# First products into the second SwiGLU in float32 from unsplit operand and weights

## The chip, the cores and the metric

The kernel runs on one core of one Trainium2 chip. The metric is the device time of one execution in microseconds, from its start to the end of the last instruction. Several runs of one kernel are given by their median. The profile is of one execution and its times count from the start of its span.

## The reference

Two layers (DEPTH = 2) work on x with 256 positions and 1024 channels. Each layer has three sublayers: a SwiGLU, three token mixers in parallel (RWKV-7, Hyena, SSD) that are merged by gates and one output projection, and a second SwiGLU. Around each stands a modulated input and a LayerNorm of the scaled residual:

```
h = x * (1 + scale) + shift            # scale, shift, gate from c, by linear layers (adaLN)
y = sublayer(h)
x = LayerNorm(ALPHA * x + gate * y)

def swiglu(h, wi, wo):                 # wi 1024 x 5632, wo 2816 x 1024
    gu = h @ wi
    return (jax.nn.silu(gu[..., :D_FF]) * gu[..., D_FF:]) @ wo
```

Everything is float32 in and out.

## The kernel before, in words

**Tiles.** Activations lie transposed: channels on the 128 partitions, positions along the row, so x is eight tiles of 128 x 256 (index m as an output, k as an input). Weights come from memory in units of [128 x 1024] float32, 512 KB: eight 128 x 128 blocks, one for each k, and a unit gives one output tile. wi's units are called here 0, 1, 2, ... in the order in which they are used: (j, q) with j the column block and q = 0 for the silu half, 1 for the other. They are issued on SyncE's queue (SP) into a ring of four raw buffers.

**Two ways of multiplying float32.** `unit` (L321) splits what has been loaded: ScalarE (ACT) writes the rounded high part (whi), VectorE (DVE) the rest (wlo), both as float32r in rings of five halves of 512 columns; the activation is split the same way (hhi, hlo). `mm3` (L341) then makes a product of three matmuls, high by high, high by low, low by high. `plain` (L311) only loads the unit, and `product` hands the float32 tiles to one matmul, which the trace shows as two records. The first `ahead` units have their own tiles in either case: wq (plain), or wqh and wql (split); the others go through the raw ring. A split unit frees its raw buffer as soon as both halves are split; a plain unit keeps it until its last product.

**The transition between two sublayers** is what the change touches. `ln_begin` (L477) starts a LayerNorm. `ln_put` (L536) is called for each of the eight output tiles of the sublayer: r = gate * psum + xa on DVE, its square on ACT, running sums racc and lsa on DVE, and at the end four matmuls of ones that add racc, lsa and the last tile and its square over the channels (tile pss). `u_put` (L500) scales r by the next sublayer's factor. `early` (L510) multiplies that not yet normalised operand with the first four units (NE = 4) of the next sublayer's first weight, in 258 columns: 256 positions and two columns that give what the mean and the shift contribute. `ln_end` (L570) takes the statistics: mean and variance (lmu, lv), the logarithm and exponential for the reciprocal root (two ACT functions with a table load between them), then for each tile r * lv, the modulated hf, and its split hhi, hlo; the units from 4 on use these. `early_end` (L525) corrects the four early results with mean and reciprocal root on DVE, and from them come the first silu (sg) and the first free psd bank.

**Which way at which transition.** From a SwiGLU into the mixers the early products are plain float32 (operand `um`). Into the second SwiGLU of a layer (from the mixers) and into the next layer's first SwiGLU they are split (operands `uh`, `ul`).

**The end of the mixers** (`mixers`, L1371): the first two branches' outputs are merged under weights pab and gates gi, in the midst of which `ln_begin` is called and the first wout unit loaded (L1428 to L1430); then a loop over eight wout units with `dense` and `ln_put` (L1435 to L1439), then `early` with the first wi units (L1440), then `ln_end` (L1442). NPRE = 1, so only unit 0 has a tile of its own. Units 4 and 5 go into psm banks, units 6 and 7 need the psd banks that early results hold until sg has read them.

**Order.** The order of the instructions on each engine, SP's queue among them, is set by a scheduler that simulates the program with its own costs; the program gives only dependences and priorities, so a change in one function moves instructions elsewhere.

Of the kernel before, what the change touches and what calls it, by code (L numbers as in the profile page):

```python
# [211 lines left out]
class Builder:  # L212
# [264 lines left out]
    def ln_begin(self, l, sub):  # L477
        self.lsub = (l, sub)
        self.nxt = (l, sub + 1) if sub < 2 else (l + 1, 0)
        self.r = self.lt("r", (8, 256))  # L480
        if (l, sub) == (0, 0):
            self.xa = self.x0
        else:
            xa = self.xa = self.lt("xa", (8, 256))
            for m in range(0, 8, 4):
                self.dma(xa[:, m:m + 4, :], self.xd[:, m:m + 4, :])
        if self.nxt in self.mods:
            mod = self.mods[self.nxt]
            if self.nxt[1] == 1:
                self.uh = self.lt("um", (8, 258))  # L490
                self.ts(self.uh[:, :, 256], mod[:, 24:32], -1.0, MUL)
                self.ts(self.uh[:, :, 257], mod[:, 32:40], 1.0, MUL)
                return
            self.uh, self.ul = (self.lt(n, (8, 258), dt=F32R) for n in ("uh", "ul"))
            ab = self.lt("uab", (8, 2))
            self.ts(ab[:, :, 0], mod[:, 24:32], -1.0, MUL)
            self.ts(ab[:, :, 1], mod[:, 32:40], 1.0, MUL)
            self.split(self.uh[:, :, 256:258], self.ul[:, :, 256:258], ab[:])

    def u_put(self, m):  # L500

        if self.nxt in self.mods:
            assert (*self.nxt, 0) in self.done and (*self.nxt, 1) in self.done
            a, hi = self.mods[self.nxt][:, 24 + m:25 + m], self.uh[:, m, 0:256]
            self.act(hi, self.r[:, m, :], AF.Identity, scale=a)
            if self.nxt[1] == 1:
                return
            self.stt(self.ul[:, m, 0:256], self.r[:, m, :], a, hi.bitcast(F32), MUL, SUB)

    def early(self, units, ahead):  # L510


        banks = [self.bank("d", 4)[:, 0:258] for _ in units]
        plain = self.nxt[1] == 1
        load = self.plain if plain else self.unit
        ws = [load(u, ahead=ahead if i < ahead else None) for i, (_, u) in enumerate(units)]
        xs = [self.uh[:, k, :] if plain else (self.uh[:, k, :], self.ul[:, k, :]) for k in range(NT)]
        for ks in (range(7), (7,)):
            for i in range(0, len(units), 2):
                for k in ks:  # L520
                    for p, w in zip(banks[i:i + 2], ws[i:i + 2]):
                        self.product(p, w, k * 128, xs[k], k == 0, k == 7)
        self.adv = [(key, p) for (key, _), p in zip(units, banks)]
# [972 lines left out]
```

## Time and profile before

| | |
|---|---|
| median of 3 runs | 1669.35 us (1665.41 to 1672.22) |
| the profiled execution | 1675.59 us |
| its span | 1673.7 us |
| mean granted clock of TensorE | 0.975 |
| busy: PE, DVE, ACT, POOL | 94%, 69%, 48%, 16% |
| from the mixers into the second SwiGLU, layer 0 | about 636 to 690 us of the span |
| the same, layer 1 | about 1445 to 1491 us |

PE is the engine of the matmuls. Its records end later than the next begins, so the distance of two starts, and not the duration shown, is what a matmul costs in a row of them. A number in square brackets behind a row of the timeline is the idle time of its engine just before it, with what ended it. PEclk is the granted clock as a share of 2.4 GHz.

### The profile page before, as it was taken

To read this page: it belongs to the slowest core of one execution; us is meant where nothing else is said; L and a number is where in the kernel's file an instruction comes from. 1 tells how busy PE (TensorE), PEld (TensorE's weight loads), DVE (VectorE), ACT (ScalarE), POOL (GpSimd) and SP (SyncE) were. 2 spreads that over 40 slices of the span, in tenths; PEclk is the share of its full clock that TensorE was granted. 3 is DMA by queue.
4 is the path that set the end of the run, shared out by engine and by line. 5 is a ranking of instruction groups with operands and counts; after the bars stand their busy time and mean duration, and the time that the engine had idled before them with its cause. 6 is when DMAs were issued, how large, how long until landed. Compare 5 with 4: busy or idle time off the path is not lost.

```text
span 1673.7 us, 31929 instructions
## 1 busy us (share of the span) xinstructions
PE 1569.5 (94%) x12118; PEld 1424.0 (85%) x12118; DVE 1150.0 (69%) x2326; ACT 801.3 (48%) x1566; POOL 267.4 (16%) x376
## 2 busy tenths in 40 slices
PE   5999999879998988899999999998999998989996
PEld 2999998768877878899999999877787787989996
DVE  6788856636446677888888887467454557876665
ACT  2655545423243535655575555452424342665554
POOL 0000013567001001100030000348620100030001
PEclk9999999989999999899999999998999999989998
DMA  9898834554548754788869986345555655666663
GB/s 376 305 324 280 282 123 155 129 127 144 169 150 288 242 170 151 282 304 295 266 220 366 315 307 199 120 106 138 156 151 158 223 188 194 189 198 221 222 177 93
DMA packets 157879, 355.74 MB, mean 213 GB/s; under 512 B 55900, under 2 KB 75805, under 8 KB 157470
## 3 DMA queue, kind: packets, MB, share of 16 engines
q1 hardware_dynamic: 157726, 353.71, 64.3%
q8 instruction: 95, 1.56, 0.4%
q14 instruction: 58, 0.48, 0.1%
HBM read 332.11 MB, written 18.91 MB: 210 GB/s over the span
## 4 chain that ended last, share of the span: by engine, by line
PE 66%; DVE 10%; POOL 9%; DMA 7%; ACT 4%; issue 3%; SPq 1%; DVEq 0%; ACTq 0%; POOLq 0%
PE psd L293 57%; PE psm L293 5%; PE pss L293 4%; POOL arena L921 3%; POOL arena L919 3%; DVE arena L282 3%; DVE arena L290 2%; DVE wlo L309 1%; SPq L296 1%; DMA arena<-in_ada 1%; ACT L279 1%; DMA gi<-gate 1%; DMA ada_raw<-in_ada 1%; ACT arena L279 1%; DMA raw<-in_pab 1%
## 5 line engine op out<-in xcount | busy, mean ns | idle before, releaser
L279 ACT ACTIVATE whi<-raw 128x512 fp32r<-128x512 f32 x608 | 370.6, 618 | 328.8 <-PE psd L293 268.2
L309 DVE TENSOR_TENSOR wlo<-raw,whi 128x512 fp32r<-128x512 f32 x608 | 405.1, 676 | 135.1 <-ACT whi L279 120.2
L293 PE MATMUL psd<-hhi,raw 128*128 128x256 f32 x1856 | 435.8, 389 | 0.7 <-DVE arena L290 0.7
L293 PEld LDWEIGHTS psd<-hhi,raw 128*128 128x128 f32 x1856 | 348.9, 192 | 63.3 <-issue 11.6
L293 PE MATMUL psd<-hhi,whi 128*128 128x256 f32 x1360 | 385.4, 285 | 9.9 <-DVE r L290 4.9
L293 PE MATMUL psd<-hhi,wlo 128*128 128x256 f32 x1360 | 384.6, 284 | 1.3 <-DVE wlo L309 1.3
L293 PE MATMUL psd<-hlo,whi 128*128 128x256 f32 x1360 | 385.5, 284 | 0.0
L293 PEld LDWEIGHTS psd<-hhi,whi 128*128 128x128 f32 x1360 | 262.0, 193 | 11.8 <-ACT sg L279 4.6
L293 PEld LDWEIGHTS psd<-hhi,wlo 128*128 128x128 f32 x1360 | 261.9, 193 | 1.6 <-DVE wlo L309 1.5
L293 PEld LDWEIGHTS psd<-hlo,whi 128*128 128x128 f32 x1360 | 262.5, 193 | 0.1
L293 PE MATMUL psd<-alo,whi 128*128 128x256 f32 x704 | 198.7, 282 | 0.0
L293 PE MATMUL psd<-ahi,wlo 128*128 128x256 f32 x704 | 197.8, 281 | 0.0
L293 PE MATMUL psd<-ahi,whi 128*128 128x256 f32 x704 | 197.4, 280 | 0.0
L581 POOL TENSOR_TENSOR r<-r,lmu 128x256 f32<-128x256 f32 x36 | 31.2, 899 | 1020.7 <-ACT lmu L279 841.3
L290 DVE SCALAR_TENSOR_TENSOR ada_raw<-ada_raw,cond 128x1024 f32<-128x1024 f32 x104 | 127.1, 1222 | 20.3 <-DMA ada_raw<-in_ada 20.1
L293 PEld LDWEIGHTS psd<-ahi,wlo 128*128 128x128 f32 x704 | 134.0, 190 | 0.3
L293 PEld LDWEIGHTS psd<-alo,whi 128*128 128x128 f32 x704 | 132.8, 189 | 0.2
L293 PEld LDWEIGHTS psd<-ahi,whi 128*128 128x128 f32 x704 | 132.2, 188 | 0.1
L293 PE MATMUL pss<-arena 128*64 128x128 f32 (+5 forms) x486 | 101.7, 385 | 26.9 <-ACT arena L279 8.6
L279 ACT ACTIVATE arena<-arena 128x512 f32<-128x512 f32 (+4 forms) x108 | 65.8, 619 | 102.5 <-DVE arena L290 35.6
L293 PEld LDWEIGHTS pss<-arena 128*64 128x64 f32 (+3 forms) x486 | 65.4, 195 | 52.1 <-issue 21.0
L293 PE MATMUL psm<-arena 32*32 32x32 f32 (+6 forms) x664 | 64.5, 263 | 28.1 <-DVE arena L290 12.6
(228 smaller groups left out, 2169.9 us busy)
## 6 DMA issues: line engine op xcount, KB each, us to landing
raw<-in_wi SPq DMA_DIRECT2D x176, 512.0 KB, 4.6
raw<-in_win SPq DMA_DIRECT2D x118, 512.0 KB, 3.8
ada_raw<-in_ada SPq DMA_DIRECT2D x104, 512.0 KB, 5.5
raw<-in_wo SPq DMA_DIRECT2D x64, 512.0 KB, 3.8
arena<-in_ada SPq DMA_DIRECT2D x32, 512.0 KB, 5.9
raw<-in_wo SPq DMA_DIRECT2D x32, 384.0 KB, 3.7
raw<-in_pab SPq DMA_DIRECT2D x24, 512.0 KB, 4.3
raw<-in_wout SPq DMA_DIRECT2D x16, 512.0 KB, 4.2
```

The lines of the kernel that those rows point to most:

```text
L279: return self.nc.scalar.activation(out=out, in_=in_, func=func, **k)
L282: return self.nc.vector.tensor_tensor(out=out, in0=a, in1=b, op=op)
L290: return self.nc.vector.scalar_tensor_tensor(out=out, in0=a, scalar=s, in1=b, op0=op0, op1=op1, **k)
L293: return self.nc.tensor.matmul(out, lhsT, rhs, start=start, stop=stop, **k)
L296: self.nc.sync.dma_start(out, in_)
L309: return self.act(hi, src, AF.Copy), (eng or self.nc.vector).tensor_tensor(out=lo, in0=src, in1=hi.bitcast(F32), op=SUB)
L581: x = sub_(out=r[:, m, :], in0=r[:, m, :], in1=mu[:], op=SUB)
L919: g.tensor_tensor(out=tv, in0=zw[:, j + 1:32, j:j + 1].to_broadcast([64, n, j]), in1=zw[:, j:j + 1, 0:j].to_broadcast([64, n, j]), op=MUL)
L921: g.tensor_tensor(out=zw[:, j + 1:32, 0:j], in0=zw[:, j + 1:32, 0:j], in1=tv, op=ADD)
```

## The change

At three places `nxt[1] == 1` (the next sublayer is the mixers) becomes true also for `nxt[1] == 2` (the next is the second SwiGLU). The transition into the next layer's first SwiGLU stays split.

```diff
@@ ln_begin
             mod = self.mods[self.nxt]
-            if self.nxt[1] == 1:
+            if self.nxt[1]:
                 self.uh = self.lt("um", (8, 258))
@@ u_put
             self.act(hi, self.r[:, m, :], AF.Identity, scale=a)
-            if self.nxt[1] == 1:
+            if self.nxt[1]:
                 return
             self.stt(self.ul[:, m, 0:256], self.r[:, m, :], a, hi.bitcast(F32), MUL, SUB)
@@ early
-        plain = self.nxt[1] == 1
+        plain = self.nxt[1] > 0
         load = self.plain if plain else self.unit
```

So in each layer the 32 early products (four units by eight k) become one float32 matmul each in the place of three float32r, ACT's eight and DVE's eight splits of half a unit and DVE's eight `ul` are gone, unit 0 is loaded into a wq tile, and units 1 to 3 stay in raw buffers until their last early product. `ln_end` splits h for the second SwiGLU as before.

**PE, layer 0, where the statistics stand among the early products.** psd 6440 to 6443 (before) and 6428 to 6431 (after) are the four early results, pss the statistics. Before, with 53 rows of early matmuls ahead of these, each a third of a product:

```order
L293 MATMUL pss_6394<-racc_6130,onesd 128x256
L293 MATMUL psd_6442<-uh_5685,wlo_6471 128x258
L293 MATMUL psd_6440<-uh_5685,wqh_6450 128x258
L293 MATMUL psd_6441<-uh_5685,whi_6460 128x258
L293 MATMUL psd_6442<-uh_5685,whi_6470 128x258
L293 MATMUL pss_6395<-lsa_6131,onesd 128x256
L293 MATMUL pss_6394<-r_5681,onesd 128x256
L293 MATMUL psd_6443<-uh_5685,whi_6476 128x258
L293 MATMUL psd_6443<-ul_5686,whi_6476 128x258
```

The statistic of lsq follows eight rows further on, and more early products after it. After, from the last wout product on:

```order
L293 MATMUL psd_6428<-um_5685,wq_6432 128x258 x5
L293 MATMUL psd_6429<-um_5685,raw_6434 128x258 x5
L293 MATMUL psd_6428<-um_5685,wq_6432 128x258
L293 MATMUL psd_6429<-um_5685,raw_6434 128x258
L293 MATMUL psd_6430<-um_5685,raw_6436 128x258 x3
L293 MATMUL pss_6383<-racc_6126,onesd 128x256
L293 MATMUL psd_6428<-um_5685,wq_6432 128x258
L293 MATMUL pss_6384<-lsa_6127,onesd 128x256
L293 MATMUL pss_6383<-r_5681,onesd 128x256
L293 MATMUL pss_6384<-lsq_6423,onesd 128x256
L293 MATMUL psd_6429<-um_5685,raw_6434 128x258
L293 MATMUL psd_6431<-um_5685,raw_6438 128x258 x3
```

All four statistics now stand behind 16 of the 32 products; the other 16 follow them, and then the products of unit 4 and 5.

**DVE, layer 0, from the last r to the first hlo.** wlo are splits of weights, lv the variance, r<-r,lv the normalised tile, hf and hlo the modulated input and its low part. Before:

```order
L309 TENSOR_TENSOR wlo_6731<-raw_6728,whi_6730 128x512
L290 SCALAR_TENSOR_TENSOR ul_5686<-r_5681,mod_5065,uh_5685 128x256
L290 SCALAR_TENSOR_TENSOR lv_6582<-pss_6395,lmu_1110_6580 128x256
L581 TENSOR_TENSOR r_5681<-r_5681,lmu_6581 128x256 x2
L309 TENSOR_TENSOR wlo_6735<-raw_6728,whi_6734 128x512
L282 TENSOR_TENSOR r_5681<-r_5681,lv_6582 128x256 x2
L287 TENSOR_SCALAR hf_6602<-r_5681,mod_5065 128x256
L282 TENSOR_TENSOR r_5681<-r_5681,lv_6582 128x256
L309 TENSOR_TENSOR wlo_6745<-raw_6742,whi_6744 128x512
L309 TENSOR_TENSOR wlo_6749<-raw_6742,whi_6748 128x512
L309 TENSOR_TENSOR wlo_6812<-raw_6809,whi_6811 128x512
L309 TENSOR_TENSOR hlo_6605<-hf_6602,hhi_6604 128x256
```

After:

```order
L290 SCALAR_TENSOR_TENSOR r_5681<-psd_6397,mod_938,xa_5682 128x256
L309 TENSOR_TENSOR wlo_6637<-raw_6634,whi_6636 128x512
L309 TENSOR_TENSOR wlo_6641<-raw_6634,whi_6640 128x512
L290 SCALAR_TENSOR_TENSOR lv_6474<-pss_6384,lmu_1094_6472 128x256
L581 TENSOR_TENSOR r_5681<-r_5681,lmu_6473 128x256 x2
L309 TENSOR_TENSOR wlo_6704<-raw_6701,whi_6703 128x512
L282 TENSOR_TENSOR r_5681<-r_5681,lv_6474 128x256 x2
L287 TENSOR_SCALAR hf_6494<-r_5681,mod_5065 128x256
L282 TENSOR_TENSOR r_5681<-r_5681,lv_6474 128x256
L309 TENSOR_TENSOR hlo_6497<-hf_6494,hhi_6496 128x256
```

The last ul and the splits of unit 4 have gone from here, those of unit 5 stand ahead of lv and the first of unit 6 behind the mean's subtraction, and no split of weights stands between r<-r,lv and the first hlo any more; unit 4 is split two r earlier.

**SP, layer 1, in the merge of the branches.** pab are the merge's weights, gi its gates, xa the residual. Before:

```order
L296 DMA xa_14744<-xd_12109 128x1024
L296 DMA gi_14621<-gate_13556 128x256
L296 DMA xa_14744<-xd_12109 128x1024
L296 DMA raw_14860<-in_pab 128x1024
L296 DMA gi_14637<-gate_13556 128x256
L296 DMA raw_14904<-in_pab 128x1024
L296 DMA gi_14663<-gate_13556 128x256
```

After:

```order
L296 DMA xa_14636<-xd_12001 128x1024
L296 DMA gi_14513<-gate_13448 128x256
L296 DMA xa_14636<-xd_12001 128x1024
L296 DMA wq_15386<-in_wi 128x1024
L296 DMA raw_14748<-in_pab 128x1024
L296 DMA gi_14529<-gate_13448 128x256
L296 DMA raw_14792<-in_pab 128x1024
L296 DMA gi_14555<-gate_13448 128x256
```

Unit 0's load stands ahead of a pab; before it stood behind the last wout load, just ahead of units 1 to 3. In layer 0 it has moved to the same region, behind the pab that stands after xa and ahead of a gi. Further on the raw ring is used in another way: units 4, 5 and 6 go one after the other through the one raw buffer that units 1 to 3 leave, and units 7 and 8 are loaded into theirs after the last early products, on SP behind three and six of the eight stores xd<-r.

## Rows read from the trace of the kernel before

**Rows 1.** The page: busy time, and the chain that ended last, by line.

```profile
PE 1569.5 (94%) x12118; PEld 1424.0 (85%) x12118; DVE 1150.0 (69%) x2326; ACT 801.3 (48%) x1566; POOL 267.4 (16%) x376
...
PE psd L293 57%; PE psm L293 5%; PE pss L293 4%; POOL arena L921 3%; POOL arena L919 3%; DVE arena L282 3%; DVE arena L290 2%; DVE wlo L309 1%; SPq L296 1%; DMA arena<-in_ada 1%; ACT L279 1%; DMA gi<-gate 1%; DMA ada_raw<-in_ada 1%; ACT arena L279 1%; DMA raw<-in_pab 1%
```

**Rows 2.** Timeline of PE, layer 0: start, duration, instruction, count, idle before.

```profile
643.24 0.36 PE L293 MATMUL psd<-hhi,whi 128*128 128x256 f32 x1 [3.32 <-DVE r L290]
...
654.01 0.28 PE L293 MATMUL psd<-uh,wqh 128*128 128x258 f32 x1
...
659.82 0.28 PE L293 MATMUL psd<-uh,whi 128*128 128x258 f32 x1
...
660.18 0.28 PE L293 MATMUL psd<-uh,whi 128*128 128x258 f32 x1
...
664.48 0.59 PE L293 MATMUL pss<-lsq,onesd 128*128 128x256 f32 x2
...
671.38 0.68 PE L293 MATMUL psm<-hhi,whi 128*128 128x256 f32 x2 [2.71 <-ACT wab L279]
...
672.87 0.58 PE L293 MATMUL psm<-hlo,whi 128*128 128x256 f32 x1 [0.80 <-DVE hlo L309]
...
681.12 0.39 PE L293 MATMUL psd<-hhi,whi 128*128 128x256 f32 x1 [1.78 <-ACT sg L279]
```

**Rows 3.** Timeline of PE, layer 1, the same two waits.

```profile
1473.58 0.74 PE L293 MATMUL psm<-hhi,whi 128*128 128x256 f32 x2 [2.71 <-ACT wab L279]
...
1483.31 0.39 PE L293 MATMUL psd<-hhi,whi 128*128 128x256 f32 x1 [1.78 <-ACT sg L279]
```

**Rows 4.** Windows: us, busy and instructions by engine, PEclk, DMA share, GB/s.

```profile
672.00:678.00 6.00, 5.20 (x25) 5.13 (x25) 5.89 (x16) 3.62 (x8) 5.31 (x5) 0.50 0.64 197
...
682.00:690.00 8.00, 8.00 (x57) 8.00 (x56) 5.47 (x14) 3.31 (x8) 0.51 (x1) 0.80 0.58 181
```

**Rows 5.** Timeline of DVE, layer 0.

```profile
665.19 0.42 DVE L290 SCALAR_TENSOR_TENSOR lv<-pss,lmu 128x256 f32<-128x256 f32 x1 [2.00 <-PE pss L293]
...
668.35 1.47 DVE L282 TENSOR_TENSOR r<-r,lv 128x256 f32<-128x256 f32 x2 [0.28 <-ACT lv L279]
...
670.40 2.08 DVE L309 TENSOR_TENSOR wlo<-raw,whi 128x512 fp32r<-128x512 f32 x3
...
687.26 1.23 DVE L290 SCALAR_TENSOR_TENSOR ada_raw<-ada_raw,cond 128x1024 f32<-128x1024 f32 x1 [1.88 <-DMA ada_raw<-in_ada]
...
688.96 1.29 DVE L309 TENSOR_TENSOR wlo<-raw,whi 128x512 fp32r<-128x512 f32 x2
```

**Rows 6.** The chain that ended last, in order of time: start, us, what.

```profile
632.61 5.64 DMA ada_raw<-in_ada
...
666.06 0.52 ACT whi L279
...
1382.67 7.38 DMA raw<-in_pab
...
1400.86 5.92 DMA arena<-hsp
```

**Rows 7.** Groups by line and form: busy, mean ns (the last from the page).

```profile
L293 PE MATMUL psd<-um,wq 128*128 128x258 f32 x128 | 28.5, 381 | 0.0
...
L290 DVE SCALAR_TENSOR_TENSOR ul<-r,mod,uh 128x256 fp32r<-128x256 f32 x24 | 11.4, 477 | 0.0
...
L279 ACT ACTIVATE whi<-raw 128x512 fp32r<-128x512 f32 x608 | 370.6, 618 | 328.8 <-PE psd L293 268.2
```

**Rows 8.** Windows: mixers' plain transition, then the merges of layers 0 and 1.

```profile
236.00:258.00 22.00, 22.00 (x108) 19.38 (x107) 12.03 (x31) 9.64 (x24) 10.73 (x14) 1.00 0.15 48
...
580.00:588.00 8.00, 6.55 (x35) 4.45 (x34) 5.24 (x11) 1.71 (x4) 0.00 (x0) 1.00 0.96 357
...
1386.00:1394.00 8.00, 5.49 (x36) 4.36 (x35) 4.26 (x8) 2.40 (x5) 0.00 (x0) 1.00 0.98 369
```

**Rows 9.** Tile raw, 630 to 690 us: loads of wi from issue to landing.

```profile
DMA to landing us min/median/max: 3.2/3.2/4.0
```

## The prediction, made before the changed kernel ran

> **What bounds the kernel now.** I read the page first, then the timeline of PE around the two transitions, then DVE and the chain there, then windows. On the page PE is busy for 94% of the span and its lines hold two thirds of the chain [rows 1]: in the SwiGLUs only a shorter PE stream or a closed gap in it saves anything. The timeline of PE shows where its gaps are. In layer 0 it waits 3.32 us for r in the wout loop, 2.71 and 0.80 us for the first normalised tiles, and 1.78 us for the silu that frees a psd bank [rows 2]. Layer 1 has the last three again, to a hundredth for the two shown [rows 3]. Behind the 2.71 us TensorE is granted 0.50 of its clock for six microseconds, and it is at 0.80 in the eight after the silu [rows 4]. A transition that is plain already, from the first SwiGLU into the mixers, has none of this: PE is busy for 22.00 of 22 us at clock 1.00 [rows 8].
>
> Who is late? In DVE's timeline the variance waits for the last statistic on PE until 665.19, the normalised tile follows at 668.35, and then DVE splits three half units of weights, 2.08 us, ahead of the first hlo [rows 5]. So the latency of the LayerNorm counts, and on it lie PE's early products ahead of the statistics and DVE's and ACT's splits.
>
> **The change, part by part.** *PE, the products.* A split product is three matmuls; starts of the same matmul follow each other in 0.36 us (659.82, 660.18) [rows 2]. A plain one is two records of 28.5 / 128 = 0.223 us [rows 7], 0.445 together. 32 products: 14.2 against 11.5, so **+2.7 us of PE a layer**, +5.4 in all. Nothing hides that if PE has no gaps left.
> By those rows float32 costs 1.25 times what the three matmuls cost. The Trainium skill, "FP8 and Floating Point Precision", section "TensorE Precision Notes", speaks against the change more strongly: true float32 is four passes through the array, the three-matmul way three, a ratio of 1.33. By that the change would add 32 x 0.12 = 3.8 us a layer, and the sum would be 2.2 us worse; the rows decide.
>
> *DVE and ACT, the splits.* Eight ul at 0.477 and eight halves at 0.69 (2.08 / 3) leave DVE, eight at 0.618 leave ACT [rows 5, 7]: 9.3 and 4.9 us a layer. DVE's are the ones that matter. In the wout loop one split leaves the place just ahead of the r for which PE waits 3.32 us; that and an ul out of two shorter waits give 1.0 us: the early products start at 653.0 instead of 654.01 [rows 2]. In layer 1 a shorter wait of the same kind gives as much.
>
> *The statistics.* Before, 664.48 - 654.01 = 10.5 us pass from the first early product to the last statistic [rows 2]. After, 16 products (7.1) and three statistics of some 0.45 (the fourth is the last) stand ahead of it: 8.4. So it starts at 661.4, 3.1 us earlier, and the variance at 662.1 instead of 665.19.
>
> *Variance to normalised tile.* 3.16 us before [rows 5], 0.52 of it a split on ACT between logarithm and table load [rows 6], which now stands ahead of the logarithm and is over by then if unit 6 has landed (a rival). 2.65 is left: 664.8. *Normalised tile to hlo's product.* 668.35 to 672.87 is 4.52 [rows 2, 5]; without the three splits, 2.08, 2.4: 667.2. PE's early products end at 653.0 + 14.2 + 1.7 = 668.9, so PE no longer waits here, and units 4 and 5 begin at full clock. *To the silu.* 672.87 to 681.12 is 8.25 [rows 2]; two splits on ACT, 1.24 [rows 7], that stand ahead of it go elsewhere: 7.0, so units 6 and 7 start at 674.2, **6.9 us earlier**. PE's 38 matmuls of units 4 and 5 last 38 x 0.12 = 4.6 from 668.9, to 673.5, so it waits 0.7 instead of 1.78.
>
> *What is late next, layer 0.* Before, the first half of unit 8 was split on DVE at 688.96, behind the work on an adaLN weight at 687.26 for whose load DVE had waited 1.88 us [rows 5]; with the split's 0.65 and the step to PE it was ready at 689.8, and PE had its work from 681.12 till then on the products ahead of it. At 0.80 of the clock [rows 4] those 8.7 us are 7.0 at full clock: PE would be there at 681.2. But that load stands on SP behind xd stores; I put its issue at 676.4, an estimate from the order and from the stores' place behind r<-r,lv. Such a load took 5.64 us [rows 6], the work on it takes 1.23 and the split 0.65 [rows 5]: 683.9, so unit 8 comes at 684.1 with the step to PE: **-5.7 us**. If the load comes in time it is -8.6; if it is as late as pab's 7.38 [rows 6] and its issue comes a microsecond later, -3.
>
> *Layer 1.* The same gaps [rows 3] give the same 6.9 us to the silu, and there is no adaLN load after it. The clock after the silu would give some 1.7 us more, and I take as much off for the raw ring: units 7 and 8 are loaded only once the last early product has freed their buffer, behind stores. **-7.0 us**, bounds -9 and -4.
>
> *Unit 0's load in the merges.* 512 KB more in a stretch where the DMA engines are taken: 0.96 at 357 GB/s in layer 0, 0.98 at 369 in layer 1 [rows 8]: 1.4 us of transfer. In layer 1 the pab behind it, 7.38 us, is on the chain, and so is arena<-hsp, 5.92 us, which moves behind a pab and two gi [rows 6]. I take **+0.5** in layer 0, where the load stands two places behind, and **+2.5** in layer 1; bounds 0 and +1.4, 0 and +4. At the place that it leaves, a load of some 3.2 us [rows 9] goes from ahead of units 1 to 3, with no wait that I count.
>
> *Nothing else.* The bytes are the same, POOL's order too. ACT is busy for 48% and its `um` takes the place of `uh`.
>
> **Sum.** -5.7 - 7.0 + 0.5 + 2.5 = **-9.7 us**; the +2.7 us a layer of PE is inside it, in the 14.2. The profiled execution, 1675.59, is 6.2 us above the median; it would become 1665.9, and the median of 1669.35 becomes **1659.7**. A difference under 0.5%, 8.35 us, is about what a measurement of this kernel can't tell from none: faster is below 1661.0, slower above 1677.7. My forecast lies just beyond that bound.
>
> **The rivals.**
> *Given back.* The gain up to the silu is real, but the merges and later loads take 5 us more than I count, half of what their bounds allow: pab and hsp up to +2.4, adaLN's load and units 7 and 8 up to +2.7 and +3.0 (-3 and -4 in the place of -5.7 and -7.0). For it speaks DMA at 0.96 to 0.98 in the merges [rows 8]; against it that the transfers after the silu are lighter, 197 GB/s [rows 4]. -9.7 + 5 = -4.7: **1664.6**. A chance of 0.24.
> *Only the swap.* The LayerNorm's latency is set by something else, so PE pays 2.7 us a layer and nothing comes earlier: +5.4, **1674.8**, within the bound. Against it: the variance waits 2.00 us for PE's last statistic, and DVE's splits stand ahead of hlo's product [rows 2, 5]. 0.08.
> *All of it.* Unit 0's load costs nothing in the merges, and adaLN's load and the raw ring are in time: -8.6 twice, **1652.2**. For it speaks the mixers' transition, which has no gap [rows 8], though with four units' own tiles; 0.12.
> *Slower: the raw ring starves the LayerNorm.* Units 4, 5 and 6 go through one buffer in series, and unit 6's split stands on ACT ahead of the variance's logarithm, unit 5's on DVE ahead of the variance. With loads of 3.2 to 4.0 us [rows 9] and splits of some 1.3 each I have unit 6 landed at 660.5, a microsecond before ACT wants it. If each of the three loads takes the 7.38 us that pab's took [rows 6], it lands 10 to 11 us later, the logarithm comes at 671 where the variance now comes at 665.19 [rows 5], PE falls idle with half the clock behind it, and each layer loses 6 instead of gaining 6: +12 +3, **1684**. It decides from the point where unit 6 lands after 666, when nothing is won. Loads between 630 and 690 never took more than 4.0 us, so 0.08.
>
> **How the numbers follow.** My forecast has 0.48, and four fifths of it and all of the third rival are faster; the rest of it, *given back* and *only the swap* lie within the bound. Faster 0.55, same 0.37, slower 0.08. The range runs from the forecast with the lower bounds and *all of it*, 1651, over *given back*, to 1670, where the gains at their smaller bounds (-3 and -4) meet the merges at their larger ones (+5.4). It leaves out *slower*, *only the swap* and the corners.
>
> **What would show each step.** In the changed profile: psd<-um,wq and psd<-um,raw in two records of 0.22 at clock 1.00; the last statistic about 8.4 us behind the first early product; no gap, or one under 0.5 us, ahead of the first psm; clock 1.00 instead of 0.50 in the six microseconds after it; unit 6 some 1 us behind the last psm product; in layer 0 a wait of some 3 us for a split behind adaLN's load; in layer 1 a pab of 8 to 9 us in the merge. I am wrong if the gap ahead of psm is still over 2 us (then something else, first of all unit 6's split, holds the LayerNorm), if a float32 record takes more than 0.25 us, or if the merges of the two layers lose more than 5 us together.

## The result, and the profile after

The changed kernel takes 1657.38 us (median of 6 runs, 1653.37 to 1660.71) against 1669.57 before (6 runs), a ratio of 0.9935 with a 95% interval of 0.9913 to 0.9956. Beside the experiments it ran once more on another chip: 1655.22 (5 runs) against 1671.11 (16 runs), 0.9904 (0.9886 to 0.9922). So it is faster by 0.65% and 0.96%, 12 and 16 us by the medians, and both intervals hold 0.9913 to 0.9922. The forecast was 1659.7 with a range of 1651 to 1670, and faster. The profiled execution took 1656.06 us, its span is 1654.3. Against the profile of before that is 19.4 us less, but 5.4 of them are there at the first matmul of layer 0's merge of the branches (psd<-yx at 565.38 before, 559.96 after), ahead of anything that the change touches: two executions of the same instructions differ that much.

The page after, its busy time and its chain by line, to be held against [rows 1]:

```profile
PE 1563.9 (95%) x12054; PEld 1415.6 (86%) x12054; DVE 1135.3 (69%) x2292; ACT 792.7 (48%) x1548; POOL 266.2 (16%) x376
...
PE psd L293 56%; PE pss L293 4%; POOL arena L921 4%; POOL arena L919 4%; PE psm L293 4%; DVE arena L290 2%; DVE arena L282 2%; DMA arena<-in_ada 1%; ACT L279 1%; DVE wlo L309 1%; ACT arena L279 1%; POOL r L616 1%; DMA raw<-in_pab 1%; DMA raw<-in_wi 1%; SPq L296 1%
```

PE has lost 5.6 us of busy time and DVE 14.7, and PE's share rises because the span fell by more. The float32 products show best in PE's timeline of layer 0 (start, duration, instruction, count, idle before), which answers to [rows 2]:

```profile
637.37 0.36 PE L293 MATMUL psd<-hhi,whi 128*128 128x256 f32 x1 [2.57 <-DVE r L290]
...
646.08 2.34 PE L293 MATMUL psd<-um,wq 128*128 128x258 f32 x10
...
648.25 2.34 PE L293 MATMUL psd<-um,raw 128*128 128x258 f32 x10
...
654.34 0.59 PE L293 MATMUL pss<-lsq,onesd 128*128 128x256 f32 x2
...
661.55 0.59 PE L293 MATMUL psm<-hhi,whi 128*128 128x256 f32 x2
...
666.94 0.39 PE L293 MATMUL psm<-hlo,whi 128*128 128x256 f32 x1 [0.43 <-DVE hlo L309]
...
668.40 0.39 PE L293 MATMUL psd<-hhi,whi 128*128 128x256 f32 x1 [0.48 <-ACT sg L279]
...
676.17 0.38 PE L293 MATMUL psd<-hhi,wlo 128*128 128x256 f32 x1 [0.31 <-DVE wlo L309]
```

Ten records take 648.25 - 646.08 = 2.17 us, 0.217 each, so a product takes 0.435 us. The last statistic starts 8.26 us behind the first early product (10.5 before). The first product of units 4 and 5 follows the last early one without a wait where PE had waited 2.71 and 0.80 us, the silu's wait is 0.48 instead of 1.78, and ahead of unit 8's low part stand 0.31 us. Inside the products of units 4 and 5 one wait of 0.43 us is left, for a later tile's low part. Layer 1 is the same to a hundredth of a microsecond [rows 3]:

```profile
1463.76 0.39 PE L293 MATMUL psm<-hlo,whi 128*128 128x256 f32 x1 [0.43 <-DVE hlo L309]
...
1465.22 0.39 PE L293 MATMUL psd<-hhi,whi 128*128 128x256 f32 x1 [0.49 <-ACT sg L279]
```

The windows (PE, PEld, DVE, ACT and POOL busy, PEclk, DMA share, GB/s) of the wout loop, the early products, units 4 and 5 and what follows the silu, then the last two for layer 1, answer to [rows 4]:

```profile
638.00:642.00 4.00, 4.00 (x36) 4.00 (x35) 3.93 (x11) 1.97 (x6) 0.00 (x0) 1.00 0.56 153
...
646.00:662.00 16.00, 16.00 (x77) 13.98 (x77) 10.88 (x19) 8.84 (x18) 6.47 (x8) 1.00 0.20 67
...
662.00:667.00 5.00, 4.47 (x33) 3.74 (x31) 5.00 (x15) 4.70 (x14) 5.00 (x6) 1.00 0.54 138
...
668.00:676.00 8.00, 7.46 (x60) 7.26 (x60) 6.60 (x16) 5.97 (x14) 0.56 (x1) 1.00 0.98 341
...
1459.00:1464.00 5.00, 4.47 (x32) 3.76 (x31) 5.00 (x15) 4.70 (x14) 5.00 (x6) 1.00 0.58 150
...
1465.00:1473.00 8.00, 7.78 (x64) 7.78 (x65) 7.24 (x17) 6.66 (x16) 0.56 (x1) 1.00 1.00 335
```

The clock is 1.00 in all of them. Before, it was 0.50 in the six microseconds of units 4 and 5, 0.80 behind the silu, and it was low in a place that the prediction had not looked at, the wout loop of layer 0 behind the wait of 3.32 us. In that place the changed kernel is not always free of it (the last section has its second profile). In the trace of the kernel before:

```profile
644.00:648.00 4.00, 4.00 (x23) 4.00 (x22) 3.08 (x8) 0.86 (x2) 0.00 (x0) 0.57 0.72 242
```

DVE in layer 0, from the variance to the first hlo and at the adaLN weight, answers to [rows 5]:

```profile
655.05 0.42 DVE L290 SCALAR_TENSOR_TENSOR lv<-pss,lmu 128x256 f32<-128x256 f32 x1 [2.78 <-PE pss L293]
...
657.08 1.21 DVE L309 TENSOR_TENSOR wlo<-raw,whi 128x512 fp32r<-128x512 f32 x1
...
658.28 1.74 DVE L282 TENSOR_TENSOR r<-r,lv 128x256 f32<-128x256 f32 x2
...
661.24 0.55 DVE L309 TENSOR_TENSOR hlo<-hf,hhi 128x256 fp32r<-128x256 f32 x1
...
673.94 1.22 DVE L290 SCALAR_TENSOR_TENSOR ada_raw<-ada_raw,cond 128x1024 f32<-128x1024 f32 x1 [1.01 <-DMA ada_raw<-in_ada]
```

No split of weights stands between 658.28 and the first hlo any more. The first of unit 6, at 657.08, is done on DVE while ACT loads its table; it takes 1.21 us where most such splits take some 0.68, while POOL works on r too, and the r<-r,lv behind it are slow as well.

### The profile page after: what moved, and what is told of

The parts are those of the page before. It is cut to its first block, busy times and chain, and to the rows that moved or that the text cites. A ratio compares the mean times of both kernels' runs of the same rounds, so it can differ in the third digit from the quotient of the medians.

```text
span 1654.3 us, 31744 instructions
## 1 busy us (share of the span) xinstructions
PE 1563.9 (95%) x12054; PEld 1415.6 (86%) x12054; DVE 1135.3 (69%) x2292; ACT 792.7 (48%) x1548; POOL 266.2 (16%) x376
## 4 chain that ended last, share of the span: by engine, by line
PE 64%; POOL 11%; DVE 9%; DMA 7%; ACT 5%; issue 3%; SPq 1%; ACTq 0%; DVEq 0%; POOLq 0%
PE psd L293 56%; PE pss L293 4%; POOL arena L921 4%; POOL arena L919 4%; PE psm L293 4%; DVE arena L290 2%; DVE arena L282 2%; DMA arena<-in_ada 1%; ACT L279 1%; DVE wlo L309 1%; ACT arena L279 1%; POOL r L616 1%; DMA raw<-in_pab 1%; DMA raw<-in_wi 1%; SPq L296 1%
## 5 line engine op out<-in xcount | busy, mean ns | idle before, releaser
L279 ACT ACTIVATE whi<-raw 128x512 fp32r<-128x512 f32 x596 | 362.8, 618 | 313.6 <-PE psd L293 243.3
L309 DVE TENSOR_TENSOR wlo<-raw,whi 128x512 fp32r<-128x512 f32 x596 | 396.3, 675 | 136.8 <-ACT whi L279 120.5
```

The source lines that it names most:

```text
L279: return self.nc.scalar.activation(out=out, in_=in_, func=func, **k)
L309: return self.act(hi, src, AF.Copy), (eng or self.nc.vector).tensor_tensor(out=lo, in0=src, in1=hi.bitcast(F32), op=SUB)
```

## The experiments

Totals of one kernel vary by 5 us and more between executions (the one before: 1666.96 to 1678.28 in 27 runs), and the merges alone by 4 (from the first of their psd<-yx to the first wout product, layer 0 took 57.0 us in one profile of the late-load kernel below and 61.4 in the other). So beside the totals I read two stretches from PE's timeline in each profile. **A0** runs from the first wout product of layer 0 to the first early product of the next transition, **A1** from the first wout product of layer 1 to the statistic of the last r in the kernel (the last pss<-r). They hold the two transitions and the SwiGLUs behind them, and hardly anything else.

| kernel | median, us | ratio to before (95%) | A0 | A1 |
|---|---|---|---|---|
| before | 1669.57 | | 232.5 | 230.0 |
| the change | 1657.38 | 0.9935 (0.9913 to 0.9956) | 223.1 | 221.0 |
| the change, again | 1655.22 | 0.9904 (0.9886 to 0.9922) | 225.0 | 221.3 |
| layer 0 only | 1663.54 | 0.9955 (0.9939 to 0.9972) | 224.6 | 227.3 |
| layer 1 only | 1662.41 | 0.9954 (0.9939 to 0.9968) | 232.9 | 222.4 |
| before, no low parts | 1656.90 | 0.9919 (0.9892 to 0.9946) | 223.6 | 223.4 |
| change, splits made again | 1670.65 | 0.9995 (0.9978 to 1.0011) | 230.9 | 227.2 |
| change, ACT's halves again | 1657.82 | 0.9919 (0.9900 to 0.9939) | 223.0 | 220.6 |
| change, DVE's ul again | 1666.08 | 0.9963 (0.9946 to 0.9980) | 226.4 | 226.1 |
| change, unit 0 loaded late | 1653.97 | 0.9908 (0.9891 to 0.9925) | 222.5 | 221.1 |
| the same, again | 1655.98 | 0.9907 (0.9888 to 0.9927) | 224.5 | 221.0 |
| change, no own tile | 1672.28 | 1.0013 (0.9995 to 1.0032) | 229.7 | 228.1 |
| change, two own tiles | 1659.06 | 0.9939 (0.9922 to 0.9957) | 225.3 | 224.9 |
| all transitions plain | 1659.20 | 0.9936 (0.9924 to 0.9949) | 224.1 | 221.4 |

By the stretches that are alike, the change saves about 8.5 us in A0 (232.5 and 232.9 against 223.1, 225.0, 224.6) and 7.1 in A1 (230.0 and 227.3 against 221.0, 221.3, 222.4), 15.6 together.

**Is it the two places, or the order of the whole program?** One transition at a time:

```diff
-            if self.nxt[1]:
+            if self.nxt[1] == 1 or self.nxt == (0, 2):
...
-        plain = self.nxt[1] > 0
+        plain = self.nxt[1] == 1 or self.nxt == (0, 2)
```

and with (1, 2) for the other.

> Plain float32 products only in layer 0's transition into the second SwiGLU; layer 1's stays split. Theory (each transition gains by its own path, DVE and ACT freed ahead of the LayerNorm, the clock kept, less 2.7 us of PE): layer 0 from its first wout product to unit 6 takes 49 us as with the whole change (57 before), layer 1 from its first wout wait to unit 6 stays at 51 us, the total falls by 6 to 8 us. Rival (the gain comes from the new order of the whole program, not from the two places): layer 0's gain does not appear alone, or the total falls by all 12 or by nothing.

> Plain float32 products only in layer 1's transition; layer 0's stays split. Theory: layer 0 keeps 57 us and the waits of 2.7 and 1.8, layer 1 takes 45 us instead of 51 and two more are saved in the SwiGLU behind it by the clock; the total falls by 5 to 8 us, and the two single changes add up to the whole one within 3 us. Rival (order of the whole program): they do not add up.

Layer 0 alone gives 7.8 us by the medians (1671.34 before in these runs), layer 1 alone 8.9, a little over the 5 to 8 expected. Each stretch is short where the change is and long where it is not. PE's timeline of the kernel with layer 0 alone: the silu's wait in layer 0 is as after, and in layer 1 the 2.71 us stand as before, though the silu's wait there is 0.59 and not 1.78.

```profile
666.89 0.39 PE L293 MATMUL psd<-hhi,whi 128*128 128x256 f32 x1 [0.49 <-ACT sg L279]
...
1460.86 0.50 PE L293 MATMUL psm<-hhi,whi 128*128 128x256 f32 x2 [2.71 <-ACT wab L279]
...
1470.11 0.39 PE L293 MATMUL psd<-hhi,whi 128*128 128x256 f32 x1 [0.59 <-ACT sg L279]
```

Measured from the first wout product to unit 6, layer 0 took 50.5 us (49 expected) and layer 1 kept 52.7 (53.2 before); with layer 1 alone it was 58.8 and 47.1 (57 and 46.4 in the two profiles that it repeats). The expectations' 51 and 45 for layer 1 count from its first wait in the loop; so counted they are 50.7 and 44.7. The two add up to 16.7, which is 4.5 us over one measurement of the whole change, more than the 3 expected, and 0.8 over the other. By the stretches each layer's gain stands by itself, and the rival falls.

**DVE's work, or the float32 matmuls?** The kernel before keeps its three float32r matmuls, but all three take high parts, and the low parts of these products are left out, so its output is not the reference's:

```diff
+            if self.nolow:
...
+                self.act(hi[:, 0:n], raw[:, o:o + n], AF.Copy)
+                parts.append((hi, hi))
+                continue
...
+            if self.nxt[1] == 2:
+                self.uh = self.ul = self.lt("uh", (8, 258), dt=F32R)
```

> The kernel before, with the low parts of operand and weights of these early products left out: three float32r matmuls stay, but all three take the high parts, so DVE's eight ul and eight splits of half a unit are gone and the output is not the reference's there; ACT, the raw ring and unit 0's late load stay as before. Theory (DVE's freed time is what counts): layer 0's 57 us fall to 48 to 50, layer 1's 51 to 44 to 46, the total by 10 to 15 us, since PE also saves its 2.7 us a layer against float32. Rival (float32 matmuls, raw weights or the early load make the gain): both stretches keep over 54 and 49 us and the total falls by less than 4.

14.4 us faster, as the change itself. Stretches from the first wout product to unit 6: 49.4 and 48.1, against 49.2 and 46.4 of the change and 56.9 and 53.2 before. Counted from the first wait the second is 46.0, the upper end of what I expected. So relief of DVE gives the gain, with no float32 matmul and with ACT's work and unit 0's load where they were. It does not come without a new order: the scheduler also puts fewer early products ahead of the last statistic, 39 and 42 of 96 matmuls in the two layers, 66 before. The next run parts the two. This one also shows that float32's price is not paid here: PE has 2.4 us a layer less to do than in the changed kernel, and nothing is faster for it. DVE's timeline there shows why:

```profile
662.44 0.68 DVE L309 TENSOR_TENSOR wlo<-raw,whi 128x512 fp32r<-128x512 f32 x1
...
663.91 0.68 DVE L309 TENSOR_TENSOR wlo<-raw,whi 128x512 fp32r<-128x512 f32 x1
...
665.88 0.67 DVE L309 TENSOR_TENSOR wlo<-raw,whi 128x512 fp32r<-128x512 f32 x1
```

Units 4 and 5 are split late, between the hlo, and unit 6 starts at 672.64, 23.3 us behind the first early product (22.3 with the change).

**The same from the other side.** The changed kernel computes what was removed, for nobody:

```diff
+        if self.nxt[1] == 2:
+            for raw in ws:
+                for o in (0, 512):
+                    hi, lo = self.t("whi", 512, 5, F32R), self.t("wlo", 512, 5, F32R)
+                    self.split(hi[:], lo[:], raw[:, o:o + 512])
...
+            self.stt(self.ul[:, m, 0:256], self.r[:, m, :], a, hi if self.nxt[1] else hi.bitcast(F32), MUL, SUB)
```

> The changed kernel, with the removed splits computed again into tiles that nobody reads: eight ul and eight low halves on DVE and eight high halves on ACT a layer, at the same places in the program. Theory: the splits are on the LayerNorm's path again and PE still pays for float32, so layer 0's stretch goes back to 55 to 60 us and the total to between 2 us below and 6 us above the kernel before. Rival (the order of statistics and the unsplit operands on PE make the gain): the total stays within 4 us of the changed kernel.

0.7 us below the kernel before, 0.9995: the gain is gone. Layer 0's stretch to unit 6 is 57.5 us, in a profile of the fastest of the ten executions (1662.61). DVE puts four splits, 2.50 us, between two r:

```profile
645.27 2.50 DVE L309 TENSOR_TENSOR wlo<-raw,whi 128x512 fp32r<-128x512 f32 x4
...
650.28 0.49 DVE L290 SCALAR_TENSOR_TENSOR r<-psd,mod,xa 128x256 f32<-128x256 f32 x1
```

PE waits for the second of these in the midst of the early products, and then has half its clock (timeline, then window):

```profile
650.82 4.67 PE L293 MATMUL psd<-um,raw 128*128 128x258 f32 x10 [2.95 <-DVE r L290]
```

```profile
651.00:655.00 4.00, 4.00 (x10) 3.16 (x11) 3.48 (x10) 3.20 (x7) 0.00 (x0) 0.50 0.42 137
```

So the last statistic starts 15.4 us behind the first early product (12.3 in layer 1) in the place of 8.3. The rival, that the order of statistics and unsplit operands make the gain, falls: the operands are there, and ahead of the last statistic stand 18 and 19 of the 32 products in the two layers, not far from the 16 of the change (before, 66 of 96 matmuls, or 22 products).

**Which part of that work?** ACT's halves alone (the lines above with only self.act), and DVE's ul alone (only the last of them):

> The changed kernel with ACT's eight removed high halves a layer computed again into tiles that nobody reads, and nothing added on DVE. Theory (DVE's time is what counts, ACT's hardly): the total stays within 3 us of the changed kernel, the stretch from the first wout product to unit 6 within 2 us of 49 and 46. Rival (ACT's 4.9 us a layer are the ones on the path): 5 us slower or more.

> The changed kernel with DVE's eight ul a layer computed again into a tile that nobody reads (3.8 of the 9.3 us that DVE lost), no splits of weights. Theory (DVE's time in the wout loop is on the path in proportion): 2 to 5 us slower than the changed kernel in all, 1 to 2.5 a layer. Rival (only the splits of weights count, which stand ahead of hlo): within 1 us of the changed kernel; rival (any DVE work there brings all back): 10 us slower.

ACT's work costs 2.6 us by the medians and nothing in the stretches: ACT is off the path. The ul cost 10.9 us by the medians, far more than the 2 to 5 expected and as much as the 10 of the rival that any DVE work there brings all back; in the stretches they cost 2 and 5 us (226.4 and 226.1 against some 224 and 221.3). The part that shows in the stretches is still more than I had priced. PE's timeline of layer 0 and a window behind the silu:

```profile
661.53 0.59 PE L293 MATMUL pss<-lsq,onesd 128*128 128x256 f32 x2
...
667.29 0.50 PE L293 MATMUL psm<-hhi,whi 128*128 128x256 f32 x2 [1.24 <-ACT wab L279]
...
674.63 0.58 PE L293 MATMUL psd<-hhi,whi 128*128 128x256 f32 x1 [1.77 <-ACT sg L279]
```

```profile
675.00:683.00 8.00, 8.00 (x57) 8.00 (x57) 5.44 (x14) 3.25 (x8) 0.56 (x1) 0.81 0.85 295
```

The statistic comes 11.3 us behind the first early product, 3.1 later than without ul. PE does not wait for it: the order puts 23 of the 32 products ahead of it instead of 16, and seven products at 0.435 are 3.0 us. So the ul count by their work and by the order that the scheduler makes with it, and this run does not part the two. The correction of the early results (wab) now stands ahead of the first hhi, PE waits for it and again 1.77 us for the silu, and the clock falls to 0.81. The rest, some 4 us of the total, is outside the stretches and I can't say from one profile whether it is the ul's. How the gain divides between the ul and the splits of weights stays open.

**Does unit 0's load cost anything in the merges?** It is kept behind the last wout load in SP's queue:

```diff
+            if self.nxt[1] == 2:
+                self.after(self.nc.sync.dma_start(raw[:, 0:width], dram), self.last)
+                return raw
...
-        self.dma(raw[:, 0:width], dram)
+        self.last = self.nc.sync.dma_start(raw[:, 0:width], dram)
```

> The changed kernel with unit 0's load kept behind the last wout load in SP's queue, out of the merges. The prediction's own price (3 us for both merges): the total falls by 2 to 4 us against the changed kernel. The theory after the result (the merges lose nothing, since their waits end on DVE and ACT and not on that load): within 2 us of the changed kernel, and the wait ahead of the merge's last matmuls stays 3.5 to 5 us in each layer.

1653.97, below the first measurement of the change by 3.4 us, but not in the same runs. So both ran again together:

> The changed kernel once more, beside the next one on the same chip. Both theories on the merges: 10 to 14 us below the kernel before.

> The changed kernel with unit 0's load kept behind the last wout load, once more, beside the changed kernel. If the load in the merges costs what the prediction said (3 us): 2 to 5 us below the changed kernel. If it costs nothing: within 1.5 us of it.

0.9904 and 0.9907, 1655.22 and 1655.98: no difference, where 2 to 5 us were expected of the prediction's price. With the first pair the late load is ahead by 1.3 us on average (1655.0 against 1656.3), and the intervals, 3 us to either side, would not show less than that. The 3 us that I had charged are not seen; 1 or 2 stay open.

The fourteen profiles of the table say where they could lie. Late in layer 1's merge, ahead of the matmuls pss<-arena, PE waits 4.05 to 6.24 us in the eight profiles with an early load there, and 2.95 to 3.60 in the six without. In layer 0 the same wait is shorter with the load, 2.62 to 3.98 us against 3.92 to 5.74, and the merges as wholes last no longer with it: 56.0 to 60.4 us against 57.0 to 62.7 in layer 0, 57.1 to 60.4 against 56.3 to 60.2 in layer 1.

**How near is the raw ring to starving the LayerNorm?** Unit 0 goes through the ring too (`early(..., 0)` in the place of `early(..., NPRE)`):

> The changed kernel with unit 0 in the raw ring too, so that all four raw buffers are held until the last early products and units 4 to 6 are loaded only then. Theory (the raw ring has a microsecond to spare with one own tile, and none without): PE waits 7 to 9 us after the early products for unit 4 (a load of 3 to 4, stores ahead of it on SP, a split of 1.3), half the clock follows, both transitions give back their gain: the total 10 to 20 us above the changed kernel, at or above the kernel before. Rival (the loads are hidden anyway): within 3 us of the changed kernel.

15 to 17 us above the two medians of the change, and no faster than the kernel before. Timeline of PE, the window behind it, and the loads of wi from issue to landing between 655 and 680 us:

```profile
668.46 0.58 PE L293 MATMUL psm<-hhi,whi 128*128 128x256 f32 x1 [6.87 <-ACT whi L279]
```

```profile
668.00:674.00 6.00, 5.54 (x26) 5.31 (x27) 5.31 (x11) 4.21 (x9) 0.00 (x0) 0.55 1.01 388
```

```profile
DMA to landing us min/median/max: 4.1/6.9/8.8
```

PE waits 6.87 us for unit 4's split (6.32 in layer 1), a little under the 7 to 9 expected, with 0.55 of the clock behind it. So the mechanism of the rival *slower* exists, and one own tile keeps it away; its price here is the whole gain, and not the 15 us beyond it of that rival's 1684. By how much is it kept away? ACT in the changed kernel:

```profile
655.58 0.63 ACT L279 ACTIVATE whi<-raw 128x512 fp32r<-128x512 f32 x1 [0.38 <-DMA raw<-in_wi]
```

Unit 6's split waits 0.38 us for its load, ahead of the variance's logarithm. I had put the load a microsecond early. It is just late.

**More own tiles, and the third transition.** Two own tiles (`early(..., 2)`), and `plain` at every transition:

> The changed kernel with own tiles for units 0 and 1, so that two raw buffers are left for units 4 to 6, and 1 MB instead of 512 KB is loaded in the merges. Theory (the ring holds up only ACT's 0.38 us wait for unit 6, and the merges are not held by such loads): within 2 us of the changed kernel, 0.5 faster. Rival (the raw ring costs the LayerNorm more than the trace shows): 3 us faster or more; rival (the merges pay for each load): 2 to 4 us slower.

> The changed kernel with the third kind of transition plain too, from layer 0's second SwiGLU into layer 1's first, with four own tiles. Theory (PE pays 2.7 us for float32; it gets back only what it waits there, 0.44 and 0.48 us ahead of the first normalised tile and the silu and 2.04 for a split behind them, and the clock is 1.00 there already): between 2 us faster and 2.7 us slower than the changed kernel, most likely 1 slower. Rival (a plain transition gains 6 to 8 us wherever it is put): 5 us faster or more.

Neither is better. With two own tiles the stretches are up to 4 us longer than with one; the statistic comes 9.6 and 10.0 us behind the first early product, since the order puts 19 and 20 products ahead of it. I did not expect that, and did not follow it up. The third transition leaves the total where it was (1659.20), as expected from a place where PE waited 0.44, 0.48 and 2.04 us and had its full clock. None of the versions beats the change beyond its interval; a ring of five raw buffers was not tried.

## Why the prediction was right, and where its steps were off

**The mechanism held.** DVE's splits and ul lay on the LayerNorm's path, and taking them away closes the gaps: the kernel without low parts shows it from one side, the one with the splits made again from the other. Their size was a term too large: 9.3 us a layer was added up from durations that partly overlap, and DVE lost 14.7 us of busy time in both layers, 7.3 in each. PE is not idle ahead of units 4 and 5, as forecast, and the last statistic's 8.4 us measured 8.26 or 8.27 wherever the change ran by itself or with unit 0's load moved.

**PE's price.** 0.445 us a product was the mean of a group whose last records run on; by the starts it is 0.435, so the price was 13.9 - 11.5 = 2.4 us a layer, not 2.7. The Trainium skill's rule ("FP8 and Floating Point Precision", "TensorE Precision Notes") of four passes for true float32 agrees with that: by an estimate of four times 258 columns at 2.4 GHz a product is 0.430 us. The ratio of 1.33 that I drew from it does not hold, because a float32r matmul takes 0.12 us, and not a fourth of 0.43; measured, it is 1.21.

**The early products start earlier than forecast.** From the first wout product to the first early one layer 0 took 26.9 us (28.1 in the second profile of the change, 28.2 with layer 0 alone) instead of 29.8: 1.6 to 2.9 less, and not 1.0. PE's waits there shrank by 1.1 to 1.4 us, from 4.0 in all to 2.9, 2.6 and 2.7. The other term, which I missed, is the clock, 0.57 for four microseconds behind the wait of 3.32: behind the 2.57 of the first profile it stays up, but in the other two it falls again, so only one of the three has that part of the gain. In layer 1, where the clock stayed at 1.00 in this stretch before too, 26.1 us became 24.1 and 24.4.

**From the variance to hlo** the two steps were too short: 658.28 - 655.05 = 3.2 us instead of 2.65, and 3.7 to hlo's product instead of 2.4. In the first, ACT's split of unit 6, late by its wait for the load, still holds up the variance's logarithm; in the second, DVE's r<-r,lv and hf are slow beside POOL's work on r. It cost nothing: PE was at its early products until 661.5 anyway. To unit 6 the saving was 7.7 us in layer 0 and 6.8 in layer 1, against the 6.9 forecast for each.

**The wait behind adaLN's load, 2.9 us, did not come.** It is 0.31 (0.84 in the second profile). The load itself was as sized, 5.90 us for 5.64, but I had put its issue 2.2 us behind unit 6 and it came 0.4 ahead (668.02 and 668.40). Before, it had been 0.7 ahead of it (680.44 and 681.12): the load and unit 6 moved together. In the chain of the changed kernel the load follows the stores, and these follow POOL's work on r:

```profile
660.86 5.77 POOL r L616 x6
...
668.02 5.90 DMA ada_raw<-in_ada
```

POOL begins it at 660.86, 0.4 us before the first hlo, where it had begun at 670.24 before. So layer 0 kept 8.5 us and not 5.7.

**The raw ring's 1.7 us in layer 1** did not come: DMA is taken fully behind the silu, 1.00 at 335 GB/s, and PE is still busy for 7.78 of 8 us.

**The merges** cost nothing that can be measured, in the place of 3.0. The pab loads of layer 1 did take 8.45 to 8.71 us from issue to landing, as the prediction had said, but the merges grew no longer by it.

So -5.7 - 7.0 + 3.0 = -9.7 was right in sign and in its largest terms. Its gaps and clock alone come to 17.2 us, and by the stretches they were worth 15.6; what I took off for later waits and for the merges, 2.9 + 1.7 + 3.0 = 7.6 us, was mostly not there. That the forecast lies only 2.3 us from the first measurement is in part luck; from the second difference, 15.9 us, it is 6.2 away. The measurements of 12 and 16 us lie between the forecast and *all of it*, whose chance of 0.12 was too small. *Given back* and *slower* fell. *Only the swap* did not happen, but the kernel with the splits made again is near to it: with DVE's work back, the exchange of matmuls alone is worth nothing that shows.

Three figures of the prediction do not follow from its own terms. Four fifths of 0.48 and the 0.12 make a chance of 0.50 for faster and leave 0.42 for the same, not 0.55 and 0.37. The smaller gains with the larger merges, -3 - 4 + 5.4, end the range at 1667.8 and not 1670. And 5 us is rather more than half of 2.4 + 2.7 + 3.0 = 8.1. None of them changes which way the result fell.

## What to carry to other kernels

Where a matmul engine waits at a LayerNorm, count what each vector instruction in front of the statistics and of the first normalised tile delays, before counting passes: a matmul form that costs PE a fifth more was free here, because it took 7 us a layer off the engine on which PE waited. A closed gap can be worth more than its length: here the clock at 0.50 behind the waits of units 4 and 5 went away with these waits. And a transfer that is moved into a busy stretch has a price only where it ends a wait; read which one before charging it. And where a scheduler orders the program, work taken off one engine also moves the others' instructions: count what stands ahead of the late one before giving the whole effect to the work.

## What the runs showed of the hardware

The clock made a difference that I had not looked for. Behind two waits of 2.71 and 0.80 us in a row it was at 0.50 for six microseconds, and without these waits it was 1.00 there. But how long a wait is does not tell by itself whether the clock falls. It was at 0.50 behind 2.95 us among the early products of the kernel with the splits made again. In the wout loop it was at 0.57 for four microseconds behind 3.32 us before; behind 2.57 it stayed at 1.00 in one profile of the changed kernel, and behind a shorter wait at the same place it fell in the other:

```profile
634.99 0.35 PE L293 MATMUL psd<-hhi,whi 128*128 128x256 f32 x1 [2.24 <-DVE r L290]
```

```profile
636.00:640.00 4.00, 4.00 (x23) 4.00 (x23) 3.84 (x11) 2.09 (x5) 0.00 (x0) 0.59 0.51 150
```

So a part of the gain, the clock in that loop, comes in some executions and not in others. 1.00 and 0.50 are TensorE's two levels, 2.4 and 1.2 GHz; a figure between them is a stretch that holds both. The Trainium skill, "TensorE: Matmul & The Clock Gate", "What's actually happening", has the low level as the default from which activity releases the engine; the rows agree, in that each drop shown stands behind a wait.

A split of half a unit on DVE, some 0.68 us elsewhere, took 1.21 at 657.08 and the two r<-r,lv behind it 1.74 instead of the 1.47 of [rows 5], while POOL worked on r. The change did not bring this. The one split that stood in the same place before, beside the same work of POOL, took as long:

```profile
666.85 1.22 DVE L309 TENSOR_TENSOR wlo<-raw,whi 128x512 fp32r<-128x512 f32 x1
```

Beside POOL (timeline of the changed kernel):

```profile
655.28 5.33 POOL L581 TENSOR_TENSOR r<-r,lmu 128x256 f32<-128x256 f32 x6 [109.04 <-ACT lmu L279]
```

In each of the two kernels' profiles there is one such slow split a layer, always beside POOL's r<-r,lmu.
